# Empty transposes around the memory's tiles, two token tiles among the memory products, rotary tables on GpSimd

## The chip, the cores and the metric

One core of a Trainium2 chip. The metric is device time in microseconds (us) of one execution. TensorE multiplies 128 x 128 blocks, ScalarE, VectorE and GpSimd work on 128 partitions, and DMA queues on the engines' sequencers (SP above all) bring data from HBM. Each engine works through a list of its own, in the order that is fixed when the program is built; semaphores make one wait for another.

## What is computed

A trunk of two layers over 1024 tokens of width 1024, in float32: layer 0 with multi-head latent attention, layer 1 with sliding-window attention. In both, four more heads attend to a normed memory of 256 rows. Cut to what the change touches:

```python
mem_n = rmsnorm(mem, mem_norm_g)
for i in range(DEPTH):
    hn = rmsnorm(x, attn_norm_g[i])
    # layer 0: proj = hn @ w_in -> c_q, c_kv, k_r, q_cross; k_r is rotated by rope(k_r, positions)
    mix, q_cross = ...
    cross = memory_cross_attention(q_cross, mem_n, w_mem_kv[i])   # kv = mem_n @ w_mem_kv[i]
    x = x + jnp.concatenate([mix, cross], axis=-1) @ w_o[i]
    x = x + squared_relu_mlp(rmsnorm(x, mlp_norm_g[i]), mlp_w_up[i], mlp_w_down[i])
return rmsnorm(x, final_norm_g)

ang = positions.astype(jnp.float32)[..., None] * inv     # rope: 16 angles for each token
cos, sin = jnp.cos(ang), jnp.sin(ang)
```

## The kernel before

Tokens are cut into eight tiles of 128 (`NT`), the width into eight blocks of 128 (`KT`). Most products take their operands as a high and a low half (`split`, lines 96 to 103: ScalarE copies the high half, VectorE subtracts for the low one) and add three partial products.

The change lies in the opening, ahead of and in the input stage of layer 0:

- `mem_T` (line 430) loads the memory's two tiles of 128 rows, gets all gains (`gains`, line 152: five small loads, one transpose, one copy into `gcol`), norms each tile (`rstd_of`: a Square with its sum on ScalarE, z on VectorE, a square root on ScalarE, Newton steps on VectorE), turns it by eight transposes into PSUM (`psTm`), and VectorE evicts four blocks at a time into `memT`, times the gain (line 445).
- `mem_kv` (line 309) multiplies `memT` with the memory weights of a layer: two key products (`pskm`, line 319) and two value products (`psvm`, line 326), plain float32. Keys are split by `dup_split` (`kmh` on ScalarE, `kml` on VectorE), values copied (`vm`). It runs for layer 0 and then for layer 1.
- The input weight `mla_w_in` comes in eight blocks through two buffers, and each is split with its gain into `wih` and `wil` (lines 102, 103).
- `rope_tables` (line 222) makes the sines and cosines of all tokens on VectorE, by range reduction in many small steps on 128 x 128 tiles, with two sines on ScalarE.
- The input stage takes the token tiles one by one: `a_norm` (norm), `a_T` (eight transposes `psT_a`, split into `xhls`), `a_in` (product `psin` with the input weight, then norms and rotation of its parts, `rope` with its last two steps on GpSimd), `a_cT` (transposes `psct` of the result). The weight of the next stage, `w_ukv`, comes through `wr` tiles and is split into `wkv` and `wkn` in between.

PSUM tiles of one bank come from `ps1`: four buffers, given out in turn in program order. `idle`, `psT_a` and the memory products all take theirs there. A framework sets the order of each engine's list when it builds the program, from priorities and its own estimate of when data is there; `tc.issue_after` makes one instruction follow another in it, and `tc.high_priority` moves one ahead. SP issues nearly all loads, in list order too.

Of the kernel before, what the change touches and what calls it, by code (L numbers as in the profile page):

```python
# [9 lines left out]
F32 = mybir.dt.float32  # L10
# [9 lines left out]
P = 128  # L20
# [35 lines left out]
def trunk(  # L56
# [38 lines left out]

    def split(src, hi, lo, scale=None):

        if scale is None:
            nc.scalar.activation(hi, src, AF.Copy)  # L99
# [27 lines left out]

    def masks(pl):

        nc.vector.tensor_copy(identb, ident)  # L130
        for dst, sgn in ((dmask, 1), (dmaskT, -1)):
# [3 lines left out]
            nc.vector.tensor_copy(dst, m)  # L135
# [16 lines left out]
    def gains(pl):  # L152
        grow = pl.tile([45, P], F32, name="grow")
        for src, r in ((mem_norm_g, 37), (attn_norm_g, 0), (mlp_norm_g, 16), (mla_q_norm_g, 32), (mla_kv_norm_g, 35)):
            n = 8 if r == 37 else src.shape[0] * src.shape[1] // P
            nc.scalar.dma_start(out=grow[r : r + n, :], in_=src.rearrange("(k p) -> k p" if len(src.shape) == 1 else "l (k p) -> (l k) p", p=P))
        pt = ps1("psg")[:, 0:45]
        nc.tensor.transpose(pt, grow, ident[0:45, 0:45])
        nc.vector.tensor_copy(gcol, pt)
# [13 lines left out]

    def newton(pl, ss, z, k):
# [3 lines left out]
        nc.scalar.activation(t, z, AF.Sqrt)  # L178
# [43 lines left out]
    def rope_tables():  # L222
        tp = pool("ropet")
        V = nc.vector
# [12 lines left out]

        def less(acc, k, c):
            V.scalar_tensor_tensor(acc, k, -c, acc, ALU.mult, ALU.add)

# [9 lines left out]
        def reduced_prod(h, c):  # L250
# [4 lines left out]
            for pc, qc in zip(parts(c, 12, 4), parts(TWO_PI, 12, 4)):  # L255
                V.scalar_tensor_tensor(acc, h, pc, acc, ALU.mult, ALU.add)
                less(acc, k, qc)
# [3 lines left out]
        with tc.issue_after(mem_end[0].ins):  # L261
            V.tensor_copy(posf, pos_i)
# [46 lines left out]
    def mem_kv(layer, kv, memT, pl):  # L309

        wsrc = w_mem_kv[layer].rearrange("(k p) n -> p k n", p=P)
        wk, wv = [pl.tile([P, KT, 256], F32, tag="wm", bufs=3, name=f"wm{layer}_{i}") for i in range(2)]
        for i, w in enumerate((wk, wv)):
            for kt in range(0, KT, 4):
                nc.sync.dma_start(out=w[:, kt : kt + 4, :], in_=wsrc[:, kt : kt + 4, i * 256 : (i + 1) * 256])
        for j in range(2):
# [3 lines left out]
            for e in range(2):  # L320
                h = 2 * j + e
                dup_split(ps[e * 64 : e * 64 + 64], kv.kh[:, h, :], kv.kl[:, h, :])
        for t in range(2):
# [3 lines left out]
            nc.scalar.activation(kv.v[:, t, :], ps, AF.Copy)  # L327
# [102 lines left out]
    def mem_T(pl):  # L430
# [5 lines left out]
        gains(pl)  # L436
# [1719 lines left out]
```

## Time and profile before

| | us |
|---|---|
| median of three runs | 2117.09 |
| lowest, highest | 2114.58, 2121.81 |
| the profiled execution | 2116.59 |
| its span, first to last instruction | 2114.9 |
| TensorE busy in it | 2078.4 (98%) |
| VectorE busy | 1470.6 (70%) |
| ScalarE busy | 1134.6 (54%) |
| GpSimd busy | 159.6 (8%) |

In rows of the trace, PE is TensorE, PEld its weight load, DVE VectorE, ACT ScalarE, POOL GpSimd, SPq and ACTq the DMA issue of SP and ScalarE. `out<-in` names tiles without their numbers: `fa` is the pair of big buffers that hold token tiles, blocks of the input weight and results of the input stage. A bracket gives the idle time before an instruction and what ended it. Busy time is no measure by itself: what counts is which engine is waited for last in a stretch.

### The profile page before, as it was taken

The page shows a single profiled execution, that of the slowest core. Times are in us where ns is not written, and L with a number is a line of the kernel's source. Part 1 is how long each engine was busy: PE and PEld are TensorE (multiplying, and loading weights), DVE is VectorE, ACT ScalarE, POOL GpSimd, SP SyncE. Part 2 cuts the span into 40 slices and gives each one's busy share as a digit, 9 for nine tenths or more (in the row PEclk, how much of TensorE's full clock was granted, in tenths as well). Part 3 has the DMA queues.
Part 4 walks back from the last instruction along what each step waited for, and adds up shares of the span by engine and source line. Part 5 has one row for each costly group of instructions (what it writes and reads, how often), then busy time and mean ns, then how long its engine had stood idle before and what let it go on. Part 6 is the DMA issues. An engine that isn't in the chain of part 4 may idle for free.

```text
span 2114.9 us, 29110 instructions
## 1 busy us (share of the span) xinstructions
PE 2078.4 (98%) x9928; PEld 1708.0 (81%) x9928; DVE 1470.6 (70%) x2833; ACT 1134.6 (54%) x2444; POOL 159.6 (8%) x224
## 2 busy tenths in 40 slices
PE   7999999999999999999999999999999999999998
PEld 6988777788788878888888878778888878788886
DVE  7555588865977776976657553866976775976565
ACT  5455477776754443444445553976745443444452
POOL 0013100001000000000001241620000000000000
PEclk9999999999999999999999999999999999999999
DMA  7202123342354446944433241242344446844342
GB/s 247 68 1 76 46 65 92 105 143 100 110 170 162 140 136 218 337 159 143 150 119 95 66 146 54 81 137 73 133 146 159 157 139 230 317 151 155 118 122 85
DMA packets 177070, 282.92 MB, mean 134 GB/s; under 512 B 17581, under 2 KB 73370, under 8 KB 176922
## 3 DMA queue, kind: packets, MB, share of 16 engines
q1 hardware_dynamic: 170480, 265.30, 39.2%
q0 software_dynamic: 4016, 13.12, 1.8%
q10 hardware_dynamic: 2426, 2.65, 0.4%
q8 instruction: 78, 1.28, 0.3%
q14 instruction: 70, 0.57, 0.1%
HBM read 187.47 MB, written 81.05 MB: 127 GB/s over the span
## 4 chain that ended last, share of the span: by engine, by line
PE 80%; DVE 7%; DMA 6%; ACT 4%; issue 2%; SPq 0%; POOL 0%; DVEq 0%; ACTq 0%; POOLq 0%
PE psy L1805 5%; PE psy L1803 5%; PE psy L1804 5%; PE psz L1805 4%; PE psz L1803 4%; PE psz L1804 4%; PE pss L930 4%; PE pso L972 4%; PE psu L1468 3%; PE psu L1470 3%; PE psu L1469 3%; DMA mr<-in_mlp_w_up_dram 3%; PE pswo L108 3%; PE pswo L110 3%; PE pswo L109 2%; PE psf L108 2%
## 5 line engine op out<-in xcount | busy, mean ns | idle before, releaser
L1368 ACT ACTIVATE mr<-mr,gcol 128x256 f32<-128x256 f32 (+1 forms) x160 | 67.3, 477 | 81.2 <-DMA mr<-in_mlp_w_up_dram 77.5
L1368 ACT ACTIVATE d<-d,gcol 128x256 f32<-128x256 f32 x128 | 57.7, 499 | 79.0 <-DMA d<-in_mlp_w_up_dram 61.7
L1803 PE MATMUL psy<-g 128*128 128x512 f32 x256 | 99.9, 390 | 0.0
L1804 PE MATMUL psy<-g 128*128 128x512 f32 x256 | 99.6, 389 | 0.0
L1805 PE MATMUL psy<-g 128*128 128x512 f32 x256 | 99.4, 389 | 0.0
L99 ACT ACTIVATE g<-i 128x512 fp32r<-128x512 f32 x79 | 49.6, 628 | 89.1 <-PE psz L1804 46.3
L100 DVE TENSOR_TENSOR g<-i,g 128x512 fp32r<-128x512 f32 x79 | 55.5, 703 | 48.9 <-ACT g L99 48.9
L99 ACT ACTIVATE uh<-i 128x512 fp32r<-128x512 f32 x66 | 41.6, 630 | 86.1 <-PE psy L1804 40.7
L99 ACT ACTIVATE i<-mr 128x512 fp32r<-128x512 f32 x78 | 49.1, 629 | 70.8 <-PE psy L1804 20.6
L951 ACT ACTIVATE p<-pss 128x512 f32<-128x512 f32 x108 | 63.6, 593 | 41.1 <-PE pss L930 41.0
L100 DVE TENSOR_TENSOR pl<-p,ph 128x512 fp32r<-128x512 f32 (+1 forms) x96 | 61.5, 651 | 27.4 <-ACT ph L99 26.9
L805 DVE TENSOR_REDUCE m<-psx 128x1 f32<-128x128 f32 (+5 forms) x96 | 70.1, 747 | 11.0 <-PE psx L801 10.8
L100 DVE TENSOR_TENSOR uh<-i,uh 128x512 fp32r<-128x512 f32 x66 | 45.6, 690 | 44.7 <-ACT uh L99 44.7
L1804 PE MATMUL psz<-g 128*128 128x512 f32 x192 | 74.7, 389 | 0.0
L1805 PE MATMUL psz<-g 128*128 128x512 f32 x192 | 74.7, 389 | 0.0
L1803 PE MATMUL psz<-g 128*128 128x512 f32 x192 | 74.7, 389 | 0.0
L100 DVE TENSOR_TENSOR i<-mr,i 128x512 fp32r<-128x512 f32 x78 | 53.6, 687 | 22.0 <-ACT i L99 21.6
L1684 DVE TENSOR_TENSOR mqf<-mqq,mqf 128x512 f32<-128x512 f32 x64 | 43.1, 686 | 21.9 <-DMA mqq<-in_mlp_w_down_dram 21.7
L99 ACT ACTIVATE ph<-p 128x512 fp32r<-128x512 f32 (+1 forms) x96 | 56.4, 599 | 1.3
L1805 PEld LDWEIGHTS psy<-g 128*128 128x128 f32 x256 | 48.1, 188 | 10.0
L1804 PEld LDWEIGHTS psy<-g 128*128 128x128 f32 x256 | 48.1, 188 | 9.9
L1803 PEld LDWEIGHTS psy<-g 128*128 128x128 f32 x256 | 48.1, 188 | 9.8
(658 smaller groups left out, 6913.4 us busy)
## 6 DMA issues: line engine op xcount, KB each, us to landing
i<-hd SPq DMA_DIRECT2D x154, 256.0 KB
hd<-uh SPq DMA_DIRECT2D x76, 256.0 KB
hd<-ul SPq DMA_DIRECT2D x76, 256.0 KB
mr<-in_mlp_w_up_dram SPq DMA_DIRECT2D x36, 512.0 KB
hd<-x SPq DMA_DIRECT2D x72, 256.0 KB
mr<-hd SPq DMA_DIRECT2D x70, 256.0 KB
d<-in_mlp_w_up_dram SPq DMA_DIRECT2D x32, 512.0 KB
mqq<-in_mlp_w_down_dram SPq DMA_DIRECT2D x32, 512.0 KB
```

The source lines that it names most:

```text
L99: nc.scalar.activation(hi, src, AF.Copy)
L100: nc.vector.tensor_tensor(lo, src, f32(hi), ALU.subtract)
L108: nc.tensor.matmul(ps, ah, bh, start=first and i == 0, stop=False)
L110: nc.tensor.matmul(ps, al, bh, start=False, stop=last and i == n - 1)
L805: nc.vector.reduce_max(m8s[h][:, i : i + 1], ps[:, c], axis=AX, negate=True)
L930: return lambda: nc.tensor.matmul(o, a, b, skip_group_check=True, **kw)
L951: nc.scalar.activation(p, ps, AF.Exp, scale=SC)
L972: mms.append(lambda: nc.tensor.matmul(o, a, b, skip_group_check=True, **kw))
L1368: nc.scalar.activation(w[:, k, :], w[:, k, :], AF.Copy, scale=g_mlp[layer][:, k0 + k : k0 + k + 1])
L1803: nc.tensor.matmul(ps, ah[:, j, :], bh, start=p in (1, 5, 2) and k == 0, stop=False, skip_group_check=True)
L1804: nc.tensor.matmul(ps, ah[:, j, :], bl, start=False, stop=False, skip_group_check=True)
L1805: nc.tensor.matmul(ps, al[:, j, :], bh, start=False, stop=k == NP - 1, skip_group_check=True)
```

## The change

- `idle(n)` issues n transposes of the identity into a PSUM tile that nobody reads: 24 at the start, 10 between the memory's two tiles, 8 behind them.
- `gains` is cut in two: the memory's gain has a load tile, a transpose (`psgm`) and a copy of its own and comes first, the other gains are turned behind the memory's tiles.
- Norms of the memory are tied to the root before them, so that the first tile's root stands ahead of the second tile's Square.
- `mem_kv` becomes a generator, `mem_kv_steps`. For layer 1, token tiles 0 and 1 are turned (`a_T`) after the key products and after the first value product. Tiles 0 and 1 are normed ahead of the weight splits, tile 2 right behind.
- The input weight takes four buffers. The loads of layer 1's memory weight stand behind its fourth block, x 2 and 3 behind all.
- `rope_tables` runs on GpSimd; each multiply-and-add is two instructions there. The sines are tied behind the last V copy, the last split copy and the last root, so they come last in ScalarE's list of this stretch.
- `masks` is made early on GpSimd; its casts follow the memory.

```diff
     def split(src, hi, lo, scale=None):
         if scale is None:
-            nc.scalar.activation(hi, src, AF.Copy)
+            ends[1] = nc.scalar.activation(hi, src, AF.Copy)
...
+    def masks_cast():
+        with tc.issue_after(mem_end[0].ins):
+            nc.vector.tensor_copy(identb, ident)
+            for dst, m in built:
+                nc.vector.tensor_copy(dst, m)
...
     def rope_tables():
-        V = nc.vector
+        V = nc.gpsimd
...
+        def add(acc, k, c):
+            n[0] += 1
+            r = tp.tile([P, NT * 16], F32, tag="add", bufs=2, name=f"rt{n[0]}")
+            V.tensor_scalar(r, k, c, None, ALU.mult)
+            V.tensor_tensor(acc, acc, r, ALU.add)
+
         def less(acc, k, c):
-            V.scalar_tensor_tensor(acc, k, -c, acc, ALU.mult, ALU.add)
+            add(acc, k, -c)
...
-        nc.scalar.activation(sinb.rearrange("p t j -> p (t j)"), th, AF.Sin)
         hs = tmp()
-        nc.scalar.activation(hs, th, AF.Sin, scale=0.5)
+        with tc.issue_after(ends[0].ins), tc.issue_after(ends[1].ins), tc.issue_after(root[0].ins):
+            nc.scalar.activation(sinb.rearrange("p t j -> p (t j)"), th, AF.Sin)
+            nc.scalar.activation(hs, th, AF.Sin, scale=0.5)
...
     def mem_T(pl):
-        gains(pl)
+        turns = [gains(pl, [mem_norm_g], 37, "m"), gains(pl, [attn_norm_g, mlp_norm_g, mla_q_norm_g, mla_kv_norm_g], 0, "")]
+        turns[0]()
         for t in range(2):
             y = pl.tile([P, D], F32, tag="y", bufs=2, name=f"ym{t}")
-            rs = rstd_of(pl, [(xs[t], D)], y)
+            with tc.issue_after(root[0].ins):
+                rs = rstd_of(pl, [(xs[t], D)], y)
             nc.vector.tensor_scalar(y, xs[t], rs[:, 0:1], None, ALU.mult)
+            if t:
+                idle(10)
...
+        turns[1]()
+        idle(8)
...
-    nc.scalar.activation(warm, eps_t, AF.Sqrt)
+    root[0] = nc.scalar.activation(warm, eps_t, AF.Sqrt)
+    def idle(n):
+        pw = ps1(f"psnone{n}")
+        for _ in range(n):
+            nc.tensor.transpose(pw[:, 0:P], ident, ident)
+
+    idle(24)
+    masks(pm)
     memT = mem_T(pm)
...
     xts = [load_x(0), load_x(1)]
+    a_norm(0)
+    a_norm(1)
...
     for kt in range(KT):
-        raw = f1[:, kt % 2, 0:MLA_IN]
+        raw = f1[:, kt % 4, 0:MLA_IN]
...
-    mem_kv(1, kvt, memT, pm)
+        if kt == 3:
+            mem1 = mem_kv_steps(1, kvt, memT, pm)
+            next(mem1)
+    xts += [load_x(2), load_x(3)]
+    for t, _ in enumerate(mem1):
+        if t < 2:
+            a_T(t)
+    a_norm(2)
+    masks_cast()
     rope_tables()
-    masks(pm)
```

Where it moves instructions, by the two programs' lists (a name carries the program's numbers: `psTm1` is the memory's tile 1, `ss3` and `zs3` belong to the norm of token tile 0, `pskm1_0` is layer 1's first key product, `psT_a0` token tile 0's transposes).

VectorE, where the memory's tiles are evicted; before:

```order
L440 TENSOR_SCALAR ym1_139<-mem1_103,rs2_144 128x1024
L445 TENSOR_TENSOR memT_100<-psTm0_0_127,gcol_73 128x4x128
L135 CAST dmaskT_68<-mask-1_411 128x128
L445 TENSOR_TENSOR memT_100<-psTm0_4_133,gcol_73 128x4x128
L445 TENSOR_TENSOR memT_100<-psTm1_0_152,gcol_73 128x4x128
L445 TENSOR_TENSOR memT_100<-psTm1_4_158,gcol_73 128x4x128
```

and with the change:

```order
L480 TENSOR_TENSOR memT_135<-psTm0_0_163,gcol_73 128x4x128
L480 TENSOR_TENSOR memT_135<-psTm0_4_169,gcol_73 128x4x128
L187 TENSOR_SCALAR zs3_296<-ss3_295 128x1
L197 RECIPROCAL rs3_299<-ss3_295 128x1
L198 TENSOR_TENSOR ss3_295<-rs3_299 128x1
L199 TENSOR_TENSOR ss3_295<-ss3_295,zs3_296 128x1
L480 TENSOR_TENSOR memT_135<-psTm1_0_199,gcol_73 128x4x128
L480 TENSOR_TENSOR memT_135<-psTm1_4_205,gcol_73 128x4x128
L173 COPY gcol_73<-psg_211 128x37
```

The four evictions stood together, with a mask cast among them; now four steps of token tile 0's norm stand before the two evictions of memory tile 1.

TensorE, from layer 1's memory products to the first input product; before:

```order
L319 MATMUL pskm1_0_267<-memT_100,wm1_0_261 128x256 x8
L319 MATMUL pskm1_1_284<-memT_100,wm1_0_261 128x256 x8
L326 MATMUL psvm1_0_301<-wm1_1_262,memT_100 128x256 x8
L326 MATMUL psvm1_1_311<-wm1_1_262,memT_100 128x256 x8
L207 MATMUL psT_a0_0_456<-ident_63,fa0_86 128x128 x4
L207 MATMUL psT_a0_4_463<-ident_63,fa0_86 128x128 x4
L207 MATMUL psT_a1_0_483<-ident_63,fa0_86 128x128 x4
L207 MATMUL psT_a1_4_490<-ident_63,fa0_86 128x128 x4
L117 MATMUL psin0_510<-wih_235,xhls_442 128x512
```

and with the change:

```order
L348 MATMUL pskm1_0_353<-memT_135,wm1_0_333 128x256 x8
L348 MATMUL pskm1_1_370<-memT_135,wm1_0_333 128x256 x8
L225 MATMUL psT_a0_0_387<-ident_63,fa0_86 128x128 x4
L225 MATMUL psT_a0_4_394<-ident_63,fa0_86 128x128 x4
L356 MATMUL psvm1_0_401<-wm1_1_334,memT_135 128x256 x8
L225 MATMUL psT_a1_0_411<-ident_63,fa0_86 128x128 x4
L225 MATMUL psT_a1_4_418<-ident_63,fa0_86 128x128 x4
L356 MATMUL psvm1_1_425<-wm1_1_334,memT_135 128x256 x8
L119 MATMUL psin0_611<-wih_319,xhls_292 128x512
```

Each token tile's transposes moved ahead of a value product.

ScalarE, around the sines; before:

```order
L280 ACT_TABLE_LOAD
L280 ACTIVATE sinb_75<-rt10_388 128x128
L102 ACTIVATE wih_235<-fa1_87,gcol_73 128x928
L327 ACTIVATE vm1_229<-psvm1_0_301 128x256
L282 ACTIVATE rt12_399<-rt10_388 128x128
L327 ACTIVATE vm1_229<-psvm1_1_311 128x256
```

and with the change:

```order
L101 ACTIVATE xhls_292<-psT_a1_0_411 128x512
L101 ACTIVATE xhls_292<-psT_a1_4_418 128x512
L357 ACTIVATE vm1_288<-psvm1_1_425 128x256
L305 ACT_TABLE_LOAD
L305 ACTIVATE sinb_75<-rt32_562 128x128
L306 ACTIVATE rt38_580<-rt32_562 128x128
L104 ACTIVATE wkvh_609<-wr128_64_0_0_907,gcol_73 128x256
L104 ACTIVATE wknh_607<-wr128_64_0_0_907,gcol_73 128x256
L104 ACTIVATE wkvh_609<-wr128_64_0_1_1036,gcol_73 128x256
L104 ACTIVATE wknh_607<-wr128_64_0_1_1036,gcol_73 128x256
```

The sines and their table moved behind the last value copy, and the high halves of the token tiles ahead of them; behind the sines stand the first splits of `w_ukv`.

## Rows read from the trace of the kernel before

**Rows 1.** Windows: length, busy us (instructions) by engine, granted clock, DMA share, GB/s.

```profile
48.00:2115.00 2067.00, 2043.05 (x9767) 1677.13 (x9766) 1435.05 (x2708) 1109.16 (x2396) 156.97 (x209) 1.00 0.41 131
...
9.90:11.00 1.10, 1.10 (x6) 1.10 (x6) 1.00 (x4) 0.00 (x0) 0.00 (x0) 1.00 1.18 325
...
13.40:20.40 7.00, 6.95 (x33) 6.11 (x33) 5.76 (x38) 4.02 (x7) 0.00 (x0) 1.00 1.05 387
...
43.00:44.00 1.00, 0.00 (x0) 0.00 (x0) 0.99 (x3) 1.00 (x1) 0.00 (x0) 0.96 0.33 131
...
50.00:51.00 1.00, 1.00 (x4) 0.85 (x4) 0.93 (x4) 1.00 (x3) 0.00 (x0) 0.63 0.01 4
```

**Rows 2.** Timeline of TensorE, memory products: start, duration, line, output, shapes, count.

```profile
13.50 7.17 PE L319 MATMUL pskm<-memT,wm 128*128 128x256 f32 x32
...
40.80 0.59 PE L326 MATMUL psvm<-wm,memT 128*128 128x256 f32 x2
...
42.19 0.63 PE L207 MATMUL psT_a<-ident,fa 128*128 128x128 f32 x4 [0.79 <-DVE kml L334]
```

**Rows 3.** Timeline of TensorE's weight loads: the first two input products.

```profile
47.56 0.34 PEld L117 LDWEIGHTS psin<-wih,xhls 128*128 128x128 f32 x1
...
59.01 0.98 PEld L207 LDWEIGHTS psT_a<-ident,fa 128*128 128x128 f32 x8
...
59.96 0.19 PEld L117 LDWEIGHTS psin<-wih,xhls 128*128 128x128 f32 x1
...
69.94 0.87 PEld L572 LDWEIGHTS psct<-ident,fa 128*128 128x128 f32 x7
```

**Rows 4.** Tile psTm (ns min/median/max), and the transposes psT_a by form, 48 to 143.

```profile
L444 PE MATMUL psTm<-ident,ym x16: 300/421/473, 9.9 to 13.2; 128*128 128x128 f32 x16
...
L207 PE MATMUL psT_a<-ident,fa 128*128 128x128 f32 x48 | 6.2, 273 | 0.0
```

**Rows 5.** Timeline of VectorE and ScalarE: memory tiles, the first token tile's norm.

```profile
12.76 1.42 DVE L445 TENSOR_TENSOR memT<-psTm,gcol 128x512 f32<-128x512 f32 x2 [0.16 <-PE psTm L444]
...
15.59 1.06 ACT L170 ACTIVATE fa<-fa 128x1024 f32<-128x1024 f32 x1 [7.99 <-DMA fa<-in_x_dram]
...
16.56 0.19 ACT L170 ACTIVATION_READ_ACCUMULATOR fa<-fa 128x1 f32 x1
...
32.90 0.21 DVE L171 TENSOR_SCALAR zs<-ss 128x1 f32<-128x1 f32 x2
```

**Rows 6.** Lines by form, 0 to 60: busy us, mean ns, idle before.

```profile
L180 DVE TENSOR_TENSOR ss<-rs 128x1 f32<-128x1 f32 x5 | 0.9, 183 | 0.1
...
L99 ACT ACTIVATE xhls<-psT_a 128x512 fp32r<-128x512 f32 x4 | 2.3, 593 | 0.0
...
L334 DVE TENSOR_TENSOR kml<-pskm,kmh 64x256 fp32r<-64x256 f32 x8 | 3.4, 422 | 0.1
...
L103 DVE SCALAR_TENSOR_TENSOR wil<-fa,gcol,wih 128x928 fp32r<-128x928 f32 x8 | 9.5, 1183 | 3.1 <-ACT wih L102 3.0
```

**Rows 7.** Waits, 0 to 60: who waited for whom, us, times, longest.

```profile
PE psT_a L207 <- DVE kml L334: 2.4, 2, 1.6
```

**Rows 8.** Lines by form of GpSimd, whole span.

```profile
L1975 POOL TENSOR_TENSOR di<-posb,pos_i 128x128 int32<-128x128 int32 x1 | 0.4, 398 | 5.1 <-PE psf L109 5.1
...
L1976 POOL CAST df<-di 128x128 f32<-128x128 int32 x1 | 0.3, 287 | 0.0
```

**Rows 9.** Timeline of GpSimd: rotary products of the input stage and of queries.

```profile
69.02 0.21 POOL L303 TENSOR_TENSOR fa<-fa,rb 128x16 f32<-128x16 f32 x1
...
205.63 0.79 POOL L303 TENSOR_TENSOR fa<-fa,rb 128x192 f32<-128x192 f32 x1
...
207.12 0.60 POOL L303 TENSOR_TENSOR fa<-fa,rb 128x192 f32<-128x192 f32 x1
```

**Rows 10.** Timeline of VectorE and ScalarE: positions landed; the square root's table.

```profile
15.10 0.17 DVE L262 CAST posf<-pos_i 128x8 f32<-128x8 int32 x1 [0.93 <-DMA pos_i<-in_positions_dram]
...
48.46 1.28 ACT L178 ACT_TABLE_LOAD   x1
```

More of the change, by code (lines that the diff above doesn't have):

```diff
@@ L150, in trunk, with gains, turn @@
     g_q, g_kv, g_mem = gcol[:, 32:35], gcol[:, 35:37], gcol[:, 37:45]
[L152 to L159, printed above, removed]
+    def gains(pl, srcs, at, name):
+        n = sum(int(np.prod(src.shape)) // P for src in srcs)
+        grow = pl.tile([n, P], F32, name=f"grow{name}")
+        r = 0
+        for src in srcs:
+            k = int(np.prod(src.shape)) // P
+            nc.scalar.dma_start(out=grow[r : r + k, :], in_=src.rearrange("(k p) -> k p" if len(src.shape) == 1 else "l (k p) -> (l k) p", p=P))
+            r += k
+        def turn():
+            pt = ps1(f"psg{name}")[:, 0:n]
+            nc.tensor.transpose(pt, grow, ident[0:n, 0:n])
+            nc.vector.tensor_copy(gcol[:, at : at + n], pt)
+        return turn
     small_ct = [0]
@@ L172, in rstd_of @@
         return newton(pl, ss, z[:, :k], k)
+    root = [None]
     def newton(pl, ss, z, k):
@@ L177, in newton @@
         rk, t = rs[:, :k], ss[:, :k]
-        nc.scalar.activation(t, z, AF.Sqrt)
+        root[0] = nc.scalar.activation(t, z, AF.Sqrt)
         nc.vector.reciprocal(rk, t)
@@ L260, in rope_tables @@
         posf = tp.tile([P, NT], F32, name="posf")
-        with tc.issue_after(mem_end[0].ins):
-            V.tensor_copy(posf, pos_i)
+        V.tensor_copy(posf, pos_i)
         ang = tmp()
@@ L309, in mem_kv, with mem_kv_steps @@
     def mem_kv(layer, kv, memT, pl):
+        for _ in mem_kv_steps(layer, kv, memT, pl):
+            pass
+    def mem_kv_steps(layer, kv, memT, pl):
         wsrc = w_mem_kv[layer].rearrange("(k p) n -> p k n", p=P)
@@ L322, in mem_kv @@
                 dup_split(ps[e * 64 : e * 64 + 64], kv.kh[:, h, :], kv.kl[:, h, :])
+        yield
         for t in range(2):
@@ L326, in mem_kv @@
                 nc.tensor.matmul(ps, memT[:, kt, t * P : (t + 1) * P], wv[:, kt, :], start=kt == 0, stop=kt == KT - 1)
-            nc.scalar.activation(kv.v[:, t, :], ps, AF.Copy)
+            ends[0] = nc.scalar.activation(kv.v[:, t, :], ps, AF.Copy)
+            yield
     def dup_split(ps, kh, kl):
@@ L485, in load_x, with a_norm, a_T @@
         return xt
+    xhls = quad_tile("q0", "xhls", F32R)
+    xT, cs_ = {}, {}
+    def a_norm(t):
+        norm_y(pa, xts[t], fa0[:, 2 + t % 2, :])
+        if 1 < t < NT - 2:
+            xts.append(load_x(t + 2))
+    def a_T(t):
+        y = fa0[:, 2 + t % 2, :]
+        xhl = [xhls[:, 2 * (t % 2) + i, :].rearrange("p (k c) -> p k c", k=KT) for i in range(2)]
+        xh, xl = xhl
+        T_split(y, lambda a: (xh[:, a : a + 4], xl[:, a : a + 4]), f"a{t}")
+        xT[t] = (xh, xl)
     xts = [load_x(0), load_x(1)]
+    a_norm(0)
+    a_norm(1)
     wih = pa.tile([P, KT, MLA_IN], F32R, name="wih")
@@ L537, in trunk @@
     CQC, CKR = 640, 896
-    xhls = quad_tile("q0", "xhls", F32R)
-    xT, cs_ = {}, {}
-    def a_norm(t):
-        norm_y(pa, xts[t], fa0[:, 2 + t % 2, :])
-        if t + 2 < NT:
-            xts.append(load_x(t + 2))
-    def a_T(t):
-        y = fa0[:, 2 + t % 2, :]
-        xhl = [xhls[:, 2 * (t % 2) + i, :].rearrange("p (k c) -> p k c", k=KT) for i in range(2)]
-        xh, xl = xhl
-        T_split(y, lambda a: (xh[:, a : a + 4], xl[:, a : a + 4]), f"a{t}")
-        xT[t] = (xh, xl)
     def a_in(t):
@@ L579, in a_cT @@
         nc.scalar.activation(krT[:, sl], pt[1][0:32, 3 * P : 4 * P], AF.Copy)
-    a_norm(0)
-    for k in range(NT + 2):
-        if k < NT:
+    for k in range(1, NT + 2):
+        if 1 < k < NT:
             a_T(k)
-        if k + 1 < NT:
+        if 1 < k < NT - 1:
             with tc.high_priority(offset=120):
```

8 lines of the change are left out of this document (5 added, 3 removed).

## Prediction

> **What bounds the kernel now.** I read the windows first. From 48 us to the end TensorE is busy 2043.05 of 2067.00 us at a granted clock of 1.00, so what is won or lost there is won or lost in TensorE's own work, which the change leaves alone [rows 1]. What can move is the stretch before 48 us, where TensorE starts late, waits and runs slow. Its end is the moment at which the first input product (psin0) is through: the weight load of the next transposes at 59.01 us [rows 3]. From there on the instruction lists of the two kernels differ only in small shifts, so I count a shift of that moment 1:1 in the total. The timeline up to it has four pieces:
>
> - The memory's products start at 13.50, when the third eviction of the normed memory ends (12.76 plus half of 1.42) [rows 2, 5]. The last one ends at 40.80 + 0.59 = 41.39: 27.9 us without a gap [rows 2].
> - 41.39 to 47.56, 6.2 us, holds only the 16 transposes of token tiles 0 and 1 [rows 2, 3]. They wait for PSUM buffers: for the low half of the memory keys, twice, 2.4 us [rows 7].
> [...]
> - psin0 takes 47.56 to 59.01, 11.45 us; the next product, from 59.96 to 69.94 at full clock, takes 9.98 [rows 3].
>
> An early slow stretch shows in durations only. The 16 memory transposes have a median of 421 ns against 273 ns for the same form later [rows 4]. Their granted clock is printed as 1.00 [rows 1], so here I go by the durations: they ran at the lower level until about 13.5, some 3.6 us after they began.
>
> **The change, part by part.** *Empty transposes.* 24 lead, 10 and 8 stand between. Before 13.5 us TensorE had nothing to do, so they cost nothing where they fit; 24 at about twice 0.12 us (eight in 0.98 at full clock, rows 3) are done by about 8 us, before the first memory tile is normed. They can make the memory transposes run at full clock. What that saves is not on the path, as the next point shows.
>
> *VectorE's order.* The two evictions of memory tile 1 now stand behind the first four steps of the norm of token tile 0, the first of which (z) needs its sum of squares. In the trace x's first tile lands so that its Square starts at 15.59 and the sum is out at 16.56 + 0.19 = 16.75 [rows 5]. SP's queue up to x is the same in both kernels, so I keep that time. The step that makes z costs 0.15, the square root on ScalarE 0.2, three small steps 0.18 each [rows 6]: about 17.75. Then the eviction, 0.71: the memory products start at 18.5 instead of 13.5. **+5.0 us.** Nothing hides it, since all of TensorE's next work reads this memory tile. Queued behind it on VectorE are the second gain copy and with it all low halves of the input weight. That the engine does not pass a waiting step by shows at 32.90: there the same sum of squares, ready at 16.75, is first used, since the step stood far back in VectorE's list [rows 5].
>
> *The clock at that start.* TensorE's last empty transposes are done by about 12 to 13 us, then it stands idle for some 5.5 us, longer than the pause after which the clock had fallen. [...] The case is nearest to unbroken work: **+1.8.** The lower bound is 0 if the clock does not fall (a rival).
>
> *Two token tiles among layer 1's memory products.* The transposes move from behind the products to between them. The pause of 6.2 us shrinks to the 16 transposes themselves, 2 × 0.95 by the load times of eight (59.01 to 59.96): **−4.3.** With no pause psin0 starts at full clock: 11.45 − 9.98, **−1.5.** A new wait: tile 1's transposes take the PSUM buffer of the second key product, and ScalarE now has two copies of tile 0 (0.59 each), a Square (1.06) and the last key pair (about 0.8) between that product's first pair (0.8) and its end; with VectorE's last pair (2 × 0.42) that is 4.7 us after the product [rows 5, 6]. TensorE gets there after eight transposes (0.95) and a V product of 3.5 (27.9/8): 4.4. **+0.4** with hand-overs.
>
> *Rotary tables on GpSimd.* VectorE loses some 60 small steps; they delayed the key pairs, and that gain is counted above. GpSimd gets 39 one-input steps, 28 two-input steps, two copies, 16 narrow steps. By 0.287 and 0.398 us, the rows of this tile size, and 0.287 for the narrow ones too [rows 8], that is 16.4 + 11.1 = 27.5 us, from 15.3 (positions landed at 15.10, rows 10) to about 43. Above: a two-input step took 0.79 instead of 0.60 beside busy VectorE [rows 9], a factor 1.3, so 51. The sines stand behind the last V copy, at about 51. **0 us**, covered by TensorE's products. If the cover is gone, ScalarE stands, with the weight splits and psin0's norm behind it.
>
> [...]
>
> *Input weight in four buffers, loads reordered on SP.* x 2 and 3 move behind the weight, and the fourth quarter of the memory weight stands ahead of its last two blocks. All of it lands some ten us before TensorE wants it in the order forecast here. 0 us. Mask casts move on VectorE: three of about 0.2 us, off the path. 0 us.
>
> **Sum.** 5.0 + 1.8 − 4.3 − 1.5 + 0.4 = **+1.4 us** (psin0 through at about 60.4). The profiled execution took 2116.59 us, 0.5 below the median of the three runs, 2117.09. So 2118.0 for a profiled run and **2118.5** as the median. 0.3% is 6.4 us, about what a measurement of this kernel can tell from no change: below 2110.7 is faster, above 2123.4 slower.
>
> **Rivals.**
>
> *A: the eviction is not held.* If x's sum is there before VectorE comes to it, the products start between 12.0 and 13.5. For it: the memory's first root no longer stands behind the second Square, so its chain is over a microsecond shorter. Against it: the Square of x waited 7.99 us for its transfer [rows 5]. Then −1.5 − 4.3 − 1.5 = −7.3: 2109.8. But TensorE would then overtake the weight: x, the input weight and layer 1's memory weight are 6.95 MB; at 387 GB/s from 13.4 [rows 1] the last block lands at 31.4. Both its splits (1.06 and 1.18) and four half pairs (0.84 each) stand before the buffer that the next V product takes: about 36.2, where TensorE arrives at 33.9. With the 0.4 that is −4.6: 2112.5.
>
> [...]
>
> *B: the input stage's tail.* The rotated key of tile 0 was ready at 69.02 + 0.21, and wanted at 69.94 [rows 3, 9]: 0.7 us to spare. Now the reload of the root's table, 1.28 us [rows 10], stands inside that chain, and the loads of w_ukv come behind the last V copy, later against psin0 by up to 3 us; for it. Against: one split pair fewer stands before the copy. 0.6 to 3.5 us more: 2119 to 2122.
>
> *C, slower: the tables come too late.* The sines are wanted at about 51; some 2 us more are free before psin0's norm is held up. From 53 on each us costs one. To pass 2123.4 they would have to end at about 58, so GpSimd would need 43 us, 1.55 times the rows' price. [...] Against: narrow steps took 0.21 us [rows 9].
>
> *D: the clock stays up* through the idle stretch, as the empty transposes would have it: 0 instead of 1.8, so 2116.7.
>
> **How the numbers follow.** The forecast 0.64; A 0.14 (0.06 at 2109.8, 0.08 at 2112.5); B 0.08; C 0.08; D 0.06. The three runs of before spread over 7 us, so a median moves by some 2 us either way: that adds 0.03 from A's upper half to faster, and 0.03 from B and the forecast's bound of 3.2 to slower. Faster 0.09, same 0.80, slower 0.11. The range 2112 to 2123 takes in both prices of the cold start, B, D and A's upper half, and leaves out A's lower half, C and the tails, a little under 0.2.
>
> **What would show it.** [...] Wrong would be: products from 12 to 13.5 (A), a ScalarE wait for GpSimd before the sines (C), a TensorE wait before the transposes of tile 0's rotated key (B), or a shift of psin0's end that the total does not repeat.

## The result and the profile after

The changed kernel takes **2127.6 us** (median of 6 runs, 2125.94 to 2130.74), the kernel before 2118.32 (6 runs): ratio 1.0047, 95% interval 1.0035 to 1.0058. It is 9.3 us slower, outside the forecast range of 2112 to 2123 and beyond the 0.3%. All medians here are of fast executions: one of 6308 us and one of 3483 us, in later runs, are left out. The profiled execution took 2127.69 us, its span is 2126.0 against 2114.9.

| moment in the trace, us | before | after | shift |
|---|---|---|---|
| first memory product starts | 13.50 | 17.85 | +4.35 |
| psin0 through (weight load of the next transposes) | 59.01 | 59.52 | +0.5 |
| last transposes of the input stage (psct) | 150.4 | 155.7 | +5.3 |
| first product of layer 0's MLP (psu) | 565.6 | 571.9 | +6.3 |
| its first down product (psy) | 854.0 | 863.6 | +9.6 |
| end of the span | 2114.9 | 2126.0 | +11.1 |

So there are two losses, one in the opening behind psin0, one far behind it, where TensorE's lists are the same in both programs. Up to psin0 the trace went as forecast. VectorE (DVE) and TensorE in the changed kernel's timeline (start, duration, ...):

```profile
16.09 0.15 DVE L187 TENSOR_SCALAR zs<-ss 128x1 f32<-128x1 f32 x1 [4.88 <-ACT fa L186]
...
17.12 1.27 DVE L480 TENSOR_TENSOR memT<-psTm,gcol 128x512 f32<-128x512 f32 x2
...
17.85 9.49 PE L348 MATMUL pskm<-memT,wm 128*128 128x256 f32 x32 [5.32 <-DVE memT L480]
...
45.32 1.04 PE L225 MATMUL psT_a<-ident,fa 128*128 128x128 f32 x8
46.20 3.62 PE L356 MATMUL psvm<-wm,memT 128*128 128x256 f32 x16
49.47 0.58 PE L119 MATMUL psin<-wih,xhls 128*128 128x512 f32 x1
```

VectorE stands for the Square of x with the eviction queued behind it, the products start at 17.85, and the first 32 take 9.49 instead of the 7.17 of [rows 2], because they start at the lower clock (19 to 23 us in the windows: granted clock 0.55, and 0.50 in each us from 18 to 22). No pause is left ahead of psin0. What went wrong stands on GpSimd (POOL), whose groups by form up to 62 us are these:

```profile
L259 POOL TENSOR_SCALAR rt<-rt 128x128 f32<-128x128 f32 x26 | 18.0, 693 | 2.0
L260 POOL TENSOR_TENSOR rt<-rt,rt 128x128 f32<-128x128 f32 x26 | 12.5, 480 | 1.5
L253 POOL TENSOR_SCALAR rt<-rt 128x128 f32<-128x128 f32 x6 | 4.2, 692 | 0.4
L289 POOL TENSOR_SCALAR rt<-posf 128x8 f32<-128x8 f32 x16 | 3.8, 239 | 0.8
L252 POOL TENSOR_SCALAR rt<-rt 128x128 f32<-128x128 f32 x6 | 2.9, 483 | 0.5
```

The table steps run from 10.66 to 60.1 us. And ScalarE (ACT), with TensorE behind it, in the timeline:

```profile
60.10 0.31 ACT L305 ACTIVATE sinb<-rt 128x128 f32<-128x128 f32 x1 [8.56 <-POOL rt L302]
...
65.00 0.51 ACT L104 ACTIVATE wkvh<-wr,gcol 128x256 fp32r<-128x256 f32 x1 [2.79 <-DMA wr<-in_mla_w_ukv_dram]
...
65.81 0.47 ACT L186 ACTIVATE fa<-psin 128x384 f32<-128x384 f32 x1
...
67.79 1.28 ACT L196 ACT_TABLE_LOAD   x1
...
73.35 1.33 PE L625 MATMUL psct<-ident,fa 128*128 128x128 f32 x7 [2.55 <-DVE fa L613]
75.31 0.40 PE L626 MATMUL psct<-ident,fa 128*32 128x128 f32 x1 [0.63 <-POOL fa L327]
```

psin0 was through at 59.5, but its Square stands behind the sines in ScalarE's list and comes at 65.81; between them stand the splits of w_ukv, one of which waits another 2.79 us for its load. TensorE runs out of work at 70.8, the clock falls once more (74 to 76 us: 0.50), and psct's last transpose stands at 75.31. Before it stood at 70.9.

### The profile page after: what moved, and what is told of

The parts are those of the page before. It is cut to its first block, busy times and chain, and to the rows that moved or that the text cites. A ratio compares the mean times of both kernels' runs of the same rounds, so it can differ in the third digit from the quotient of the medians.

```text
span 2126.0 us, 29219 instructions
## 1 busy us (share of the span) xinstructions
PE 2087.6 (98%) x9971; PEld 1711.9 (81%) x9971; DVE 1460.1 (69%) x2770; ACT 1135.4 (53%) x2444; POOL 204.4 (10%) x314
## 3 DMA queue, kind: packets, MB, share of 16 engines
q8 instruction: 78, 1.28, 0.3%
## 4 chain that ended last, share of the span: by engine, by line
PE 75%; DMA 9%; DVE 7%; ACT 5%; POOL 2%; issue 2%; SPq 0%; DVEq 0%; ACTq 0%; POOLq 0%
PE psy L1855 5%; PE psy L1857 5%; PE psy L1856 5%; PE psz L1856 4%; PE psz L1855 4%; PE psz L1857 4%; PE pss L982 4%; DMA mr<-in_mlp_w_up_dram 3%; PE pso L1024 3%; PE psu L1520 3%; PE psu L1522 3%; PE psu L1521 3%; DMA d<-in_mlp_w_up_dram 3%; PE psf L110 2%; PE psf L112 2%
## 5 line engine op out<-in xcount | busy, mean ns | idle before, releaser
L101 ACT ACTIVATE i<-mr 128x512 fp32r<-128x512 f32 x78 | 49.1, 629 | 69.7 <-PE psy L1856 25.7
L1954 POOL TENSOR_TENSOR wsr<-wsr,gcol 128x1024 f32<-128x1024 f32 x12 | 23.4, 1949 | 359.3 <-DMA wsr<-in_swa_w_in_dram 333.8
L1857 PEld LDWEIGHTS psy<-g 128*128 128x128 f32 x256 | 48.0, 188 | 10.0
L1855 PEld LDWEIGHTS psy<-g 128*128 128x128 f32 x256 | 48.1, 188 | 9.9
```

The source lines that it names most:

```text
L101: ends[1] = nc.scalar.activation(hi, src, AF.Copy)
L1855: nc.tensor.matmul(ps, ah[:, j, :], bh, start=p in (1, 5, 2) and k == 0, stop=False, skip_group_check=True)
L1857: nc.tensor.matmul(ps, al[:, j, :], bh, start=False, stop=k == NP - 1, skip_group_check=True)
```

## The experiments

"Shift" is that of the last psct transposes against the kernel before (150.4), from the profile. "Rest" is the difference of the medians less that shift: what happens behind the input stage. It mixes runs with one profile and is uncertain by some 2 to 3 us: two rows are of the same kernel ("evictions first, fast, 16 more" and "the same again") and differ by 1.4 us, and where the profiled execution was an unusual one, its own rest is another. That of the change with 16 more is +4.0 by its profile (a span 10.0 us longer, less the 6.0), not -0.8. "Empty" counts TensorE's products beyond those of before (9928 on the page).

| run | empty | us | before | ratio, 95% | shift | rest |
|---|---|---|---|---|---|---|
| the change | 43 | 2127.60 | 2118.32 | 1.0035 to 1.0058 | +5.3 | +4.0 |
| tables on VectorE | 43 | 2122.42 | 2117.93 | 1.0013 to 1.0032 | +0.6 | +3.9 |
| evictions first | 43 | 2127.31 | 2117.93 | 1.0028 to 1.0063 | +6.3 | +3.1 |
| both | 43 | 2121.00 | 2117.93 | 1.0007 to 1.0026 | +1.3 | +1.8 |
| sines late | 43 | 2123.44 | 2117.93 | 1.0017 to 1.0040 | +3.2 | +2.3 |
| evictions first, sines late | 43 | 2123.50 | 2118.46 | 1.0014 to 1.0032 | +3.6 | +1.4 |
| second operation added | 43 | 2120.13 | 2118.46 | 0.9997 to 1.0019 | +0.6 | +1.1 |
| evictions first, fast steps | 43 | 2119.14 | 2118.87 | 0.9995 to 1.0013 | -2.6 | +2.9 |
| before, empties alone | 43 | 2124.93 | 2118.46 | 1.0022 to 1.0046 | +5.4 | +1.1 |
| before, 43 small | 43 | 2118.13 | 2117.96 | 0.9990 to 1.0008 | -0.9 | +1.1 |
| tables on VectorE, no empties | 4 | 2119.35 | 2118.46 | 0.9996 to 1.0015 | +0.5 | +0.4 |
| the change, 16 small more | 59 | 2123.19 | 2117.96 | 1.0011 to 1.0035 | +6.0 | -0.8 |
| tables on VectorE, 16 more | 59 | 2118.93 | 2118.87 | 0.9990 to 1.0013 | +2.7 | -2.6 |
| evictions first, fast, 16 more | 59 | 2115.11 | 2118.87 | 0.9977 to 0.9997 | -1.2 | -2.6 |
| the same again | 59 | 2114.76 | 2117.96 | 0.9979 to 0.9997 | -2.0 | -1.2 |
| before, 59 small | 59 | 2113.14 | 2117.96 | 0.9971 to 0.9993 | -3.3 | -1.5 |
| tables on VectorE, 56 more | 99 | 2118.83 | 2118.87 | 0.9985 to 1.0008 | +3.2 | -3.2 |

### What holds the opening

Tables on VectorE:

```diff
-        V = nc.gpsimd
+        V = nc.vector
...
-            add(acc, k, -c)
+            V.scalar_tensor_tensor(acc, k, -c, acc, ALU.mult, ALU.add)
```

In this run, and in all others with the tables on VectorE, the cast of the positions is also tied behind the memory's last eviction.

> The rotary tables' steps on VectorE again, one instruction for a multiply-and-add; all the rest as changed, the sines still queued last. Theory T (GpSimd's table steps, over at 60.06 us, hold ScalarE's list at the sines by 8.56 us, which makes 4.8 of the 5.3 us lost by the end of layer 0's input stage): the sines wait for less than 1 us, the transposes of the first rotated key come at about 71.5 instead of 75.31, and the end of the input stage is within 1 us of the kernel before; the total is then 2118 to 2120 if the other 4 us, lost behind 450 us, were scatter, and about 2122 if they belong to the change. Theory E (the eviction behind token tile 0's norm, which starts the memory products 4.3 us late, is what costs): no gain, still 5 us late, about 2127.

The shift falls from 5.3 to 0.6, with the products starting at 17.48, nearly as late as in the change. T holds, E falls. ScalarE waits 0.25 us for the tables instead of 8.56:

```profile
51.82 0.31 ACT L300 ACTIVATE sinb<-rt 128x128 f32<-128x128 f32 x1 [0.25 <-DVE rt L297]
```

The total keeps 3.9 us behind the input stage, so that part is not scatter of one profile.

Evictions first:

```diff
-    a_norm(0)
-    a_norm(1)
+    with tc.issue_after(mem_end[0].ins):
+        a_norm(0)
+        a_norm(1)
```

> The norms of token tiles 0 and 1 tied behind the last eviction of the memory, all the rest as changed, the tables on GpSimd. Theory T: the memory products start between 12 and 13.5 us instead of 17.85 and psin0 is through 3 to 5 us earlier, but the table steps still end at about 60, ScalarE waits for them as before, now with TensorE idle for longer behind psin0, and the total moves by less than 1.5 us: 2126 to 2128. Theory E: all of it comes through, 4 to 5 us less than the changed kernel: about 2123.

The products start at 12.37, the total is the same, as T had it: ScalarE now waits 10.74 us for the tables, which end at 59.9. The late start, the largest term of the sum, cost nothing while the tables bound the stage.

Both edits:

> Both edits: tables on VectorE, and the norms tied behind the last eviction of the memory. Theory T: products start at 12 to 13.5, nothing holds the sines, so psin0 is through 3 to 5 us earlier than in the kernel before, and the total is 2112 to 2116, 2 to 6 us less than the kernel before. Theory E: the same gain as in the run with the second edit alone, about 2123. If the weight's splits bind TensorE, as one rival of the prediction worked out, 2112.5 is the floor.

T missed: it asked for 2112 to 2116. The shift is +1.3, not a gain: TensorE overtakes the weight, as rival A worked out. It waits for a PSUM buffer, 4.39 us where that rival had 2.3. By the order in which the buffers are given out it is the one of the key product whose last pair (`kml`) VectorE ends at 39.71, behind two splits of the weight and some table steps (start, duration on VectorE, then on TensorE):

```profile
35.84 1.18 DVE L105 SCALAR_TENSOR_TENSOR wil<-fa,gcol,wih 128x928 fp32r<-128x928 f32 x1
...
39.28 0.43 DVE L360 TENSOR_TENSOR kml<-pskm,kmh 64x256 fp32r<-64x256 f32 x1
...
39.81 6.44 PE L351 MATMUL psvm<-wm,memT 128*128 128x256 f32 x16 [4.39 <-issue]
```

Sines late (the angles lie in `sinb` and `cosb` themselves, and the sine of the half angle comes first; only the place of the call is shown):

```diff
+            with tc.issue_after(root[0].ins):
+                sines()
         rope(pa, ps[:, 640:672]...
```

> Tables on GpSimd as changed, but the two sines stand behind the root of psin0 in ScalarE's list (the angles are kept in the tables' own tiles), so that nothing but the rotation of the key stands behind them. Theory T: table steps end at about 60 as before, no instruction of ScalarE waits for them by more than 1 us, the square of psin0 comes at about 60.5 instead of 65.81, and the transposes of the rotated key at 71 to 72.5 instead of 75.31; 3 to 5 us less than the changed kernel by the end of the input stage: 2122 to 2124 if the 4 us behind 450 us stay. Theory B (the reloads of the root's and the sine's table and the later loads of w_ukv are what costs): the reload stays and now stands fully in the chain, so the transposes stay at 74 to 76 and the total at 2126 to 2128.

2 us of the 5.3 are gone and the total is in T's range, but T's picture was incomplete: it allowed no wait over 1 us. ScalarE still waits, one instruction further on:

```profile
60.07 0.51 ACT L104 ACTIVATE wknh<-wr,gcol 128x256 fp32r<-128x256 f32 x1 [6.24 <-POOL sinb L303]
```

A half of w_ukv waits for the last table step. It reads nothing of the tables; by the program it lies where the tables' scratch tiles were given back. That reuse as the cause is read from the code, not tried. Rival B of the prediction falls: the root's table load of 1.28 us also stands behind psin0 in the run with a second operation, where the shift is 0.6.

Evictions first and sines late:

> Norms of token tiles 0 and 1 tied behind the memory's last eviction, and the sines behind the root of psin0; tables on GpSimd as changed. Theory T (GpSimd's table steps matter only through ScalarE's list): with the list free, the earlier start of the memory products comes through: psin0 starts at 47 us as in the run with the evictions first, its square follows at about 58, the rotated key's transposes at 69 to 71; layer 0's input stage ends 1 to 3 us before the kernel with the sines late alone (which was 3.2 us late), so 0 to 2 us late against the kernel before. The total follows with the 2 to 4 us that all four kernels of this opening have lost behind 450 us: 2120 to 2123. If GpSimd's end at about 60 still binds (the rotation needs the sines, and its last steps stand in GpSimd's list), the transposes of the rotated key stay at 72 and the total at 2123 to 2124.

psin0 starts at 45.2, but that same split waits 10.14 us, so the gain of the start is lost again: GpSimd's end at 60 binds at this split, too.

### Why the steps were slow

A second operation, adding zero, in the 32 steps that had a single one:

```diff
-            V.tensor_scalar(r, k, c, None, ALU.mult)
+            V.tensor_scalar(r, k, c, 0.0, ALU.mult, ALU.add)
...
-            V.tensor_scalar(r, r, -MAGIC, None, ALU.add)
+            V.tensor_scalar(r, r, -MAGIC, 0.0, ALU.add, ALU.add)
```

> The changed kernel, with a second operation (adding zero) in each of GpSimd's table steps that had one: 32 steps. In the changed kernel's trace a step with two operations took 0.30 us and one with a single operation 0.53. Theory T with the form of the step as its cause: these steps come down to about 0.30 us where VectorE doesn't disturb them, the tables end some 5 to 7 us earlier, at 53 to 55 instead of 60.06, ScalarE waits 2 to 4 us instead of 8.56, and the total falls by 2.5 to 5 us to 2122.5 to 2125. Rival: the 0.53 belongs to the place (what VectorE does beside them), not to the form; the steps stay at 0.5 us and the total at 2126 to 2128.

By line (ns min/median/max), in the changed kernel:

```profile
L259 POOL TENSOR_SCALAR rt<-rt x26: 527/529/1418, 16.9 to 57.7; 128x128 f32<-128x128 f32 x26
L252 POOL TENSOR_SCALAR rt<-rt x6: 297/298/932, 15.9 to 53.9; 128x128 f32<-128x128 f32 x6
```

and with the second operation:

```profile
L259 POOL TENSOR_SCALAR rt<-rt x26: 300/300/1084, 17.1 to 53.0; 128x128 f32<-128x128 f32 x26
L253 POOL TENSOR_SCALAR rt<-rt x6: 644/664/1583, 16.4 to 50.1; 128x128 f32<-128x128 f32 x6
```

By the medians of these rows the form decides: a multiplication followed by an addition takes 0.30 us, a single operation 0.53, two additions 0.66. The tables end at 55.1, ScalarE's wait falls to 3.47 us, and the shift to 0.6:

```profile
55.11 0.31 ACT L305 ACTIVATE sinb<-rt 128x128 f32<-128x128 f32 x1 [3.47 <-POOL rt L302]
```

5 us sooner was enough, since only what ends behind psin0 counts. The median falls by 7.5 us, more than the 2.5 to 5 forecast: 4.7 of them are the shift, and 2.8 lie behind the input stage, where nothing was changed. They are not explained; four of the ten executions took over 2122 us, the profiled one 2123.35.

Evictions first, and both kinds of step as multiply-and-add (times 1, or plus 0):

```diff
-            V.tensor_scalar(r, r, -MAGIC, None, ALU.add)
+            V.tensor_scalar(r, r, 1.0, -MAGIC, ALU.mult, ALU.add)
```

> The changed kernel with the norms of token tiles 0 and 1 tied behind the memory's last eviction, and GpSimd's one-operation table steps written as a multiplication and an addition (times 1 or plus 0). Theory T and the form of the step: both kinds take 0.30 us undisturbed (0.53 in the changed kernel; in the run with two additions 0.66), the tables are over at about 50 us, ScalarE waits for them by less than 3 us, and with the memory products from 12 to 13.5 us psin0 starts at 45 to 47; the rotated key's transposes come at 68 to 69, 2 to 3 us before the kernel before. Total 2116 to 2119, since the steps in the MLP stages stay as in the other kernels of this opening. If the wait for PSUM buffers (3.3 us at 37.5 in the runs with the evictions first) grows, the opening comes out even and the total at 2119 to 2121.

All these steps have a median of 0.30 us now. The tables end at 53.1, later than the 50 forecast, since single steps still stretch to 1.1 or 1.25 us, and ScalarE waits 5.97 us where less than 3 was forecast. The opening is 2.6 us ahead of the kernel before and the total even with it, so 2.9 us go behind it, as expected.

### What is lost behind the opening

Tables on VectorE, and one empty transpose at each place:

```diff
-        for _ in range(n):
-            nc.tensor.transpose(pw[:, 0:P], ident, ident)
+        nc.tensor.transpose(pw[:, 0:P], ident, ident)
```

> Tables on VectorE as in the first run, and only one empty transpose in place of 24, 10 and 8 at each place. Theory H (the 42 empty transposes and the extra gain transpose lengthen TensorE's list, so that the fetches of its instructions fall at other moments for the rest of the program, on top of loads of MLP weights): the loss behind 450 us, 3.7 us with the tables on VectorE, shrinks to under 1.5 us, and the total comes to 2118.5 to 2120. Rival N (that loss has to do with the start of the stages or is scatter): it stays at 3 to 4 us, total 2121 to 2123. In the opening, the transposes of the memory run at the lower clock again and end up to 2 us later, which the wait for the square of x hides.

2119.35 instead of 2122.42, with the opening as late: the rest falls from 3.9 to 0.4. H is favoured, but with this edit the framework also ordered the opening anew (psin0 starts at 37.4, between the memory products).

The kernel before with the empty transposes alone:

```diff
+    for i in range(4):
+        pw = ps1(f"psnone{i}")
+        for _ in range(11 if i < 3 else 10):
+            nc.tensor.transpose(pw[:, 0:P], ident, ident)
     memT = mem_T(pm)
```

> The kernel before with 43 empty transposes ahead of the memory's, where TensorE waits until 9.66 us anyway; nothing else is changed. Theory H: the opening stays within 0.5 us (perhaps up to 0.7 us earlier, since the memory's transposes run at the higher clock), and the rest of the program loses 2 to 4 us: 2120 to 2122. Rival N: 2117 to 2118.5, no loss behind 450 us.

A miss: the framework answered the 43 transposes with another order, and the opening lost 5.4 us. The rest is +1.1 by the medians and +4.5 by the profiled execution, the slowest of the six, so this run does not tell H from N.

So the next edits add transposes of 8 x 8, which cost 0.55 us for 16 and move the framework's order less. To the kernel with the tables on VectorE, first 16, then 56 of them:

```diff
         idle(8)
+        pw = ps1("psnone_small")
+        for _ in range(16):
+            nc.tensor.transpose(pw[0:8, 0:8], ident[0:8, 0:8], ident[0:8, 0:8])
```

> Tables on VectorE as in the first run, and 16 more empty transposes of 8 x 8 behind the last 8, where TensorE waits 4.9 us for the eviction anyway. Nothing else is changed, so by what TensorE computes nothing should move. Theory H (the transfers of TensorE's instructions, one for some 256 of them, slow a load of MLP weight that has been issued 1 to 2.6 us before): 32 more instructions bring each transfer some 3.7 us earlier against the program. In the first run three of them fell 1 to 2.1 us behind loads (638.38, 1674.5, 1733.6), which took 4.9 to 5.4 us instead of 3.9 to 4.6, and each was followed by a step of about 1 us in the shift against the kernel before; with 16 more none falls there, those three loads take 4.2 to 4.7 us, the three steps are gone, and the total comes to 2119 to 2121. Rival N (the loss behind 450 us has another cause or is scatter): the steps stay at the same loads, and the total at 2122 to 2123.

> The same with 56 more small transposes instead of 16. Theory H: each transfer comes some 13 us earlier, and about five of them fall 2 to 2.7 us behind loads between 655 and 780 us (659, 687, 718, 745, 776 by the first run's times), none on 638, 1674 or 1733: the steps of about 1 us stand at other loads, the product of MLP 0 loses 2 to 4 us against the kernel before, later in the stage than in the first run, and MLP 1 nothing. Total 2120 to 2123. Rival N: the steps stay at the loads of the first run.

Sixteen empty transposes take 3.5 us off the total although the opening is 2.1 us later: the rest goes from +3.9 to -2.6. With 56 it is -3.2, and the total, 2118.83, lies below H's 2120 to 2123. N, which kept the steps and the time, falls. Of H's details some came and some did not: with sixteen the three steps are gone, but others of about 1 us came at the loads of 610, 668 and 727 us, each with a transfer 1.2 to 1.3 us behind its issue. Layer 0's MLP loses 1.1 us against the kernel before instead of 2.6; layer 1's, where the kernel before itself has such a step at 1708 us, wins 1.5 instead of losing 0.5.

The same three lines behind `idle(24)`, in the kernel with evictions first and fast steps:

> The run before this one with 16 more empty transposes of 8 x 8 behind the first 24, where TensorE waits for the memory's first tile. Theory H: the opening is the same to 0.5 us, and the steps at the three loads (638, 1674 and 1733 by the first run's times) are gone: 1.5 to 3 us less than without them, 2114 to 2117, below the kernel before. Rival N: the same time as without them.

4.0 us less than without the sixteen, although the opening is 1.4 us later: more than H's 1.5 to 3, and below the kernel before. Run again:

> The kernel with the evictions first, the fast table steps and 16 more small transposes once more, for a narrower interval: 2114 to 2117, a ratio to the kernel before of 0.998 to 0.9995. By rival N it was scatter, and the ratio comes to 1.000 to 1.001.

Both intervals lie below 1 (0.9977 to 0.9997, 0.9979 to 0.9997).

The change itself with the same three lines, sixteen more:

> The changed kernel itself with 16 more empty transposes of 8 x 8 behind the last 8, where TensorE waits for the eviction anyway; tables on GpSimd, sines queued last, as changed. Theory H (the count of TensorE's instructions decides on which MLP loads the transfers of its instructions fall): what the changed kernel lost behind 450 us is gone, 3 to 6 us less than the changed kernel, 2122 to 2125; the steps at the loads of 645, 1680 and 1740 us (its own times) are gone; what is left against the kernel before is the opening's 5 us. Rival N: the same as the changed kernel, 2126 to 2129.

2123.19: 4.4 us less, with the opening 6.0 us late. By the medians, what the change lost behind the input stage is won back; the six executions fall into two groups, 2120.7 to 2121.8 and 2124.6 to 2126.6, and the profiled one is the slowest. Its trace shows that the loss is not undone where it arose. Shift gained in each MLP (565 to 850 us and 1590 to 1900 us of the kernel before, the same products in both profiles):

| kernel | layer 0's MLP, without and with 16 more | layer 1's MLP, without and with |
|---|---|---|
| the change | +2.9, +2.6 | +0.8, -1.1 |
| tables on VectorE | +2.6, +1.1 | +0.5, -1.5 |
| evictions first, fast | +1.5, +2.8 | +0.4, -4.0 |
| the same again, with 16 more only | +2.4 | -1.4 |

Only in layer 1's MLP do all three pairs win. In layer 0's MLP of this run the step at the load of 645 us is gone, and three others stand at the loads of 612, 671 and 729 us. The last two rows are of one kernel: its -4.0 and -1.4 show how far two executions differ.

The count of TensorE's instructions and what moves them, from the changed kernel's page (busy us, share and instructions by engine; a DMA queue's packets, MB and share):

```profile
PE 2087.6 (98%) x9971; PEld 1711.9 (81%) x9971; DVE 1460.1 (69%) x2770; ACT 1135.4 (53%) x2444; POOL 204.4 (10%) x314
...
q8 instruction: 78, 1.28, 0.3%
```

Queue q8 moves instructions: 78 transfers for 9971 products and as many weight loads, one for about 256 (that they are TensorE's is taken from this count). Between 590 and 800 us they come every 25 to 34 us. The place of one load in the changed kernel (SPq is SP's issue), then the DMA queues from 644.7 to 650.2:

```profile
644.72 0.38 SPq L1443 DMA_DIRECT2D d<-in_mlp_w_up_dram  x1
...
650.21 0.91 ACT L1420 ACTIVATE d<-d,gcol 128x256 f32<-128x256 f32 x2 [4.54 <-DMA d<-in_mlp_w_up_dram]
...
653.34 0.58 ACT L1559 ACTIVATE i<-psu 128x512 f32<-128x512 f32 x1
...
653.97 0.50 PE L1520 MATMUL psu<-mqf,x 128*128 128x512 f32 x1 [0.59 <-ACT i L1559]
```

```profile
q8 instruction: 1, 0.02, 1.4%
```

and the same load with sixteen more:

```profile
643.77 0.38 SPq L1446 DMA_DIRECT2D d<-in_mlp_w_up_dram  x1
...
647.69 0.91 ACT L1423 ACTIVATE d<-d,gcol 128x256 f32<-128x256 f32 x2 [2.97 <-DVE x L1586]
```

In the changed kernel the transfer falls 2.3 us behind the load's issue, and ScalarE's first step on the load, which waits for the landing, starts 5.49 us after it. An eviction of PSUM stands behind that step, and TensorE waits for the eviction. With sixteen more the transfer falls 0.5 us behind the issue, and ScalarE starts on the load after 3.92 us. Over both MLP stages of all 18 profiles, and the loads of `mlp_w_up` for which a wait of ScalarE ended with the landing: 48 with a transfer 0.9 to 2.5 us behind the issue landed after a median of 4.8 us, 523 with none from 1 us ahead to 5 us behind after 4.0. Each of the 48 took longer than the median of the same load in the profiles that have no transfer beside it, by 0.1 to 1.8 us, median 0.8. A transfer 0.5 to 0.9 us behind the issue did no such thing (11 loads, median -0.4).

In the changed kernel's profile three steps stand at such loads (645, 1680 and 1740 us): 0.8, 1.1 and 0.9 us. That is 2.8 of the 5.8 us that this profile loses behind the input stage; for the rest no such transfer is found.

The kernel before with such lines ahead of `mem_T`, 43 and then 59:

> The kernel before with 43 empty transposes of 8 x 8 ahead of the memory's, where TensorE waits until 9.66 us: its list is then as long as that of the changed kernel. The planner moves some steps of the opening for it, so the opening may shift by up to 5 us either way; what counts is the shift from the end of the input stage to the end. Theory H: 2 to 4 us lost there against the kernel before, with steps of about 1 us at the loads of 637, 1673 and 1732 us (by the kernel before's times), as in the changed kernel. Rival N: under 1 us.

A miss on the total: the rest is +1.1. TensorE's products are as many as in the change, but in layer 0's MLP the transfers come 1.6 us earlier against the program (0.7 us behind the load of 636.7), so no step stands there. At the load of 1727.8, with a transfer 1.4 us behind, there is a step of 0.7 us, as H had it. Equal counts of products are not equal lists.

> The same with 59 small transposes, a list as long as that of the runs with 16 more. Theory H: no steps at those loads; 2 to 3 us won against the kernel before from the end of the input stage to the end, as in those runs (by their medians they won 2.7 to 2.8 us there). If the opening keeps within 1 us, 2115 to 2117. Rival N: within 1 us of the kernel before there.

2113.14, the fastest of all, but mostly by its opening: with a new order on ScalarE and VectorE the input stage ends 3.3 us earlier. The rest is -1.5 by the medians, between the two theories, and -3.0 by the profile.

What stays open: that the transfer itself slows the load is seen by where both fall, not by a run that moves the transfer alone. A step of up to 1.3 us at the load of 588 us (594 in the changed kernel, where it is 0.9) has no transfer behind it. In five of the profiles (tables on VectorE, both, second operation added, and two with 16 more) another step of 1.6 us stands at the products `psf` near 1320 us, far from these loads, and is not explained. And the rest scatters by 2 to 3 us among kernels whose lists on TensorE are equally long: +1.1 with the second operation added, +4.0 in the change.

## Why the prediction was wrong

**Start of the products, +5.0:** 17.85 instead of 18.5, +4.35 (x landed 0.7 us earlier, its Square began at 14.91). Right, and rival A falls. **Clock at that start, +1.8:** 9.49 - 7.17 = 2.3. Right in its direction, and D falls. No run shows the 1.8 itself, nor the bound of 3.2; in their place the windows of the changed kernel show a granted clock of 0.50 from 16 to 22 us and of 0.71 from 22 to 23, with the products running from 17.85. The memory's transposes, behind the empty ones, had a median of 273 ns, 421 before [rows 4]. **The pause, -4.3, and psin0 at full clock, -1.5:** both came; from 17.85 TensorE doesn't pause until psin0 is through, and psin0 takes 10.1 us, all at a granted clock of 1.00, instead of 11.45 (in the kernel before the windows give 0.50 from 44 to 50 us and 0.63 from 50 to 51). **PSUM wait, +0.4:** none; tile 1's transposes follow at once. Together +0.5 at psin0's end where +1.4 was forecast. These terms were right, but they did not decide the total.

**"0 us, covered" for the tables failed.** 27.5 us were forecast, with 51 as the latest end. The 39 one-input steps took 25.7 us (18.0 + 4.2 + 2.9 + 0.6) instead of 11.2, the 28 two-input steps 13.4 instead of 11.1, and 5 us passed between steps. Two things were mis-sized. The price of 0.287 came from a cast [rows 8], while 32 of the 39 are single operations, which take 0.53 undisturbed; by the medians of the changed kernel's own rows (0.53, 0.30, 0.46 and 0.64) the 67 steps cost 32 us, not 22. And the 5 us between the steps were put at nothing. The factor of 1.3 for a step beside a busy VectorE, though taken from one pair of rows [rows 9], was not too low: 39.1 us against those 32 are 1.2. Single steps stretched much further: the step at L253 that began at 19.91 took 1.47 us, beside two splits of the weight on VectorE (1.17 us from 19.82, 1.16 from 20.98); at 16.27 and 18.43, ahead of the splits, steps of that line took 0.55 and 0.53. So **rival C** came, which had 0.08: it asked for 43 us from 15.3, and the tables took 49 from 10.66.

**"I count a shift of that moment 1:1 in the total" failed too.** It is the sentence that the list of signs at the end named as a way to be wrong. TensorE's lists behind the opening are the same, yet 4 us more were lost there. What the runs show in place of the 1:1: 43 more products on TensorE ahead of the lists move where its instruction transfers fall (one at 648.2 us before, at 647.05 in the change, where layer 0's MLP starts 6.3 us later), loads of MLP weights with a transfer 0.9 to 2.5 us behind their issue land 0.8 us later, and sixteen products more change the total by 3.5 to 4.4 us. How much of the 4 us is owed to this stays open: the three steps at such loads make 2.8 of the profile's 5.8 us. TensorE works on without a gap through the transfer at 647.05 us (busy for all of 647.0 to 647.5); it is the load beside it that lands late (ScalarE starts on it 5.49 us after its issue, 3.92 with sixteen more). The prediction had priced the empty transposes by their own time alone.

Of the 9.3 us, 5.3 are lost in the input stage, and that is the tables: 32 steps with a second operation, or the tables on VectorE, take it to 0.6. The other 4 lie behind it. Sixteen empty transposes win as much by the medians, but not at the places where it was lost.

## What to carry to other kernels

Price a step on another engine by a row of that very form and operation count, and add the time between the steps; then follow every queue and every buffer that waits for the last of them. A term that is covered has to be checked against its cover at the upper price, since here the early terms of the sum (the late start, the clock) didn't matter at all. Where a stage waits for its loads, as the MLPs do here, instructions added ahead can change the time far behind them (here sixteen took 3.5 to 4.4 us off): compare two lengths of the list before a small difference is put down to the edit, and look whether the loss and the gain stand at the same place.

## What was not expected of the hardware

On GpSimd a 128 x 128 step with a multiplication and an addition took 0.30 us, with one operation alone 0.53, with two additions 0.66 (medians), with a maximum and a minimum 0.64. Sixteen empty transposes of 0.55 us in all changed the total by 3.5 to 4.4 us in three pairs of kernels. A load with an instruction transfer 0.9 to 2.5 us behind its issue landed 0.8 us later (median of 48) than the same load without one.
